# SSD scan of a hybrid decoder step: decays fetched after their exponential, differences on VectorE, GpSimd's weight remainders in pieces, three projections in a layer's first group

## The chip, the cores and the metric

The kernel runs on one core of a Trainium2 chip: TensorE (PE; its weight loads are PEld), VectorE (DVE), ScalarE (ACT), GpSimd (POOL) and SyncE (SP), which issues the DMAs. The metric is the device time in microseconds of one execution. The median of three runs of the kernel before is 2900.59 us (2896.8 to 2905.93).

## The reference

Two layers. Each layer takes 1024 prompt tokens and 32 sample tokens (8 sequences of 4), 1024 wide, through

```python
u = rms_norm(x, norm_mix)
q, k, v, z, xbc, dt = split(u @ w_in)              # 512, 128, 128, 1024, 1536, 16 columns
xbc = silu(causal_conv(xbc, width 4))              # x: 16 heads of 64;  B, C: 2 groups of 128 states
y = ssd_scan(x, softplus(dt + dt_bias), -exp(a_log), B, C, state) + d_skip * x
x = x + concat([attention(q, k, v), rms_norm(y * silu(z))]) @ w_out
x = x + (silu(g) * up) @ w_down                    # FFN, 2816 wide
```

The scan works in chunks of 128 tokens. Within a chunk, with `acum` the running sum of `dt * A` and s, q two tokens of it,

```python
decay   = exp(where(q >= s, acum[q] - acum[s], -inf))
y_intra = (C B^T * decay) @ (x * dt)
states  = B^T (x * dt * exp(acum[end] - acum));  h = h * exp(acum[end]) + states
y_inter = (C @ h_before) * exp(acum)
```

## The kernel before

Activations lie transposed: 128 columns of the model on the partitions, the 1056 tokens along the free axis in three tiles of 352. Each projection of 128 output columns is, for one tile, 8 (or 4, or 5) blocks k of three matmuls (`mm3`, L280 to L295): weights and activations are split into a high part rounded to fp32r and a low remainder, and hi·hi, hi·lo and lo·hi are added up in one PSUM bank of tag `g` (three of them). A tile of a projection is thus 24 matmuls of 128x352.

**Weights.** `load_next` (L252) fetches a block (tag `w`, 5 buffers), ScalarE casts it to `whi` (L266, 3 buffers), and GpSimd subtracts for the remainder (L267), in one instruction for all 8 blocks k. `weights(key)` keeps one weight prepared ahead.

**Order.** The program is written tile by tile; a planner orders the instructions of each engine with its own model of durations, and each engine then runs its queue in that order. `Flow` mixes the work around the projections: after each tile of a projection, `flow.tick()` advances one or two of the open generators by one `yield`. `issue_after` pins something behind a given instruction.

**Start.** The rows of x are fetched (L209), squared on ScalarE (L473), transposed on TensorE (L467) and copied out (L479), a reciprocal root is iterated on VectorE (`rsqrt`, L305 to L311), and per block k VectorE scales (L485), ScalarE casts to `ahi` (L486) and VectorE or GpSimd takes the remainder `alo` (L487; in tile 0 four of eight on GpSimd). This is written in the functions `roots`, `columns` and `first_norm`, the squares of tile 1 ahead of the norm of tile 0. In layer 1 the same comes from `norm_end` (L351 to L356, its splits at L244 and L248) behind the last down projection (L373).

**Projections.** `proj` (L556) takes one or more columns blocks and goes over the three tiles, all blocks of a tile before the next tile. The first group is dt (`d`, 16 columns, L289) with block x10 (C of group 0); then x8 (B of group 0) by itself; then x0, x1 and so on. A conv block leaves PSUM on ScalarE (L657), is weighted on ScalarE and VectorE (L667, L669), and gets its Silu on ScalarE (L670). A z block takes its Silu on ScalarE (L860), multiplies y on VectorE (L864), and squares on ScalarE (L868) with the sum on GpSimd (L869).

**Steps.** `steps` (L572, pushed behind the first group) computes softplus and the running sums; the transposed sums go to DRAM as `acd` (L613).

**Scan.** `ssd(j)`, j = 0 to 7 per layer, treats two heads in five `yield`s. In the first two, one for each half hf of 512 tokens: fetch `acd` of both heads broadcast over the partitions into `bc` (tag F1, 512 KB); transpose y (L728); two VectorE products with `wdec` and `dt` (L732); eight ScalarE Relus of 128x128 (L738), which make `max(acum[s] - acum[q], 0)` into `tt` (tag F2); its exponential (L739), the exponential of `bc` (L740, 128x1024), GpSimd's product of `bc` with C (L741, 128x1024), VectorE's product of `tt` with the masked C B^T (L742). The third computes the chunk states (matmuls L748) and the running state H (L753, L758). The fourth adds the intra part into a PSUM bank per half (L767, 64 stationary columns a head), the fifth adds the inter part into the same banks (L778, per chunk and head 64 columns of H against 128 columns of `bc`), and VectorE puts d_skip * x + PSUM into y (L780). TensorE shows two matmul records for each fp32 matmul.

After the scan: `stream` (the sample states, L832 to L846), `gnorm` (L872), `prep` (L685), attention (L1116 to L1260), the out projection (`one_ssm`, whose sum is L1271), and the FFN.

Of the kernel before, what the change touches and what calls it, by code (L numbers as in the profile page):

```python
# [10 lines left out]
F32 = mybir.dt.float32  # L11
# [7 lines left out]
L = 2  # L19
# [141 lines left out]
def body(ctx: ExitStack, tc, A, outs):  # L161
# [90 lines left out]
    def load_next():  # L252

        k, (fill, nk, cw) = wlist.popleft()
        raw = mk("w", [P, nk, cw], bufs=WB)
        load[0] = fill(raw)
        if cw == 16:

            both = mk("whi", [P, nk, 32], F32R, bufs=3)
            SC.copy(both[:, :, 0:16], raw)  # L260
            G.tensor_tensor(both[:, :, 16:32], raw, both[:, :, 0:16].bitcast(F32), op=ALU.subtract)
            wready[k] = both, None
            return
        hi = mk("whi", [P, nk, cw], F32R, bufs=3)
        lo = mk("w", [P, nk, cw], F32R, bufs=WB)
        SC.copy(hi, raw)  # L266
        G.tensor_tensor(lo, raw, hi.bitcast(F32), op=ALU.subtract)  # L267
        wready[k] = hi, lo
# [136 lines left out]
    acd = [dr.tile([16, S], F32, name=f"acd{l}") for l in range(L)]  # L405
# [53 lines left out]
    sizes = [[P if b < 8 else NS for b in range(3 * t, 3 * t + 3)] for t in range(NT)]  # L459

    def blocks(t):
        return slice(3 * t * P, 3 * t * P + sum(sizes[t]))

    def rows_to_columns(t, src):
        pt = pbank()
        for i, m in enumerate(sizes[t]):
            TE.transpose(pt[:, i * P:i * P + m], src(i)[0:m], ident[0:m, 0:m])  # L467
        return pt[:, 0:sum(sizes[t])]

    def roots(t):  # L470
        for i, m in enumerate(sizes[t]):
            sq = slot("F1", [P, D])
            SC.activation(sq[0:m], xr[3 * t + i][0:m], AF.Square, accum_out=s9[0:m, 3 * t + i:3 * t + i + 1])  # L473
        return rsqrt("r3", s9[:, 3 * t:3 * t + 3], D, bufs=2)

    def columns(t):
        for k in range(KD):
            pt = rows_to_columns(t, lambda i: xr[3 * t + i][:, k * P:(k + 1) * P])
            (SC.copy if k % 2 and t else V.tensor_copy)(x[k][:, blocks(t)], pt)  # L479

    def first_norm(t, y):
        SC.copy(rb[:, blocks(t)], rows_to_columns(t, lambda i: y[:, i:i + 1].to_broadcast([P, P])))
        for k in range(KD):
            s = mk("nu", [P, TW], bufs=3)
            V.scalar_tensor_tensor(s, x[k][:, tsl(t)], g_mix(0, k), rb[:, tsl(t)], op0=ALU.mult, op1=ALU.mult)  # L485
            hi = SC.copy(u[0][t][:, k, :], s)  # L486
            (V if k % 4 == 3 or (k % 2 and t == 0) else G).tensor_tensor(u[1][t][:, k, :], s, u[0][t][:, k, :].bitcast(F32), op=ALU.subtract)  # L487
        return hi

    y = roots(0)  # L490
    columns(0)
    y1 = roots(1)
    hi = first_norm(0, y)
    columns(1)

    with tc.issue_after(hi.ins):
        y2 = roots(2)
    first_norm(1, y1)
    columns(2)
    first_norm(2, y2)  # L500
# [54 lines left out]
    for l in range(L):  # L555
# [16 lines left out]
        def steps():  # L572
# [38 lines left out]
            acT = s2[:, 0:P]  # L611
            V.tensor_copy(acT, pt[:, 0:P])
            SY.dma_start(out=acd[l].rearrange("h (c q) -> (h c) q", q=P), in_=acT)  # L613
# [103 lines left out]
        def ssd(j):  # L717
# [3 lines left out]
            bcs, tts, xds, pys = {}, {}, {}, {}  # L721
            for hf in range(2):
                sl = slice(hf * 512, hf * 512 + 512)
                bc = bcs[hf] = slot("F1", [P, 2, 512])
                SY.dma_start(out=bc, in_=acd[l][2 * j:2 * j + 2, sl].partition_broadcast(P))
# [8 lines left out]
                tt = tts[hf] = slot("F2", [P, 2, 512])  # L734
# [26 lines left out]
            for hf in range(2):  # L761
                tt, xd2 = tts[hf], xds[hf]
                py = pys[hf] = pbank()
                for c in range(4):
                    q = slice(c * P, (c + 1) * P)
                    for hh in range(2):
                        TE.matmul(py[hh * 64:hh * 64 + 64, q], lhsT=xd2[:, 0, c, hh, :], rhs=tt[:, hh, q],  # L767
                                  start=(c == 0), stop=False)
            yield
            for hf in range(2):  # L770
                sl = slice(hf * 512, hf * 512 + 512)
                py, bc = pys[hf], bcs[hf]
                for c in range(4):
                    ci = hf * 4 + c
                    q = slice(c * P, (c + 1) * P)
# [117 lines left out]
        def z(j):  # L893
# [5 lines left out]
             conv(10, ct))  # L899
        flow.push("steps", steps())  # L900
        proj(conv(8, bt))
# [527 lines left out]
```

## Time and profile before

| | |
|---|---|
| median of three runs | 2900.59 us |
| the profiled execution | 2900.49 us |
| its span, first to last instruction | 2898.6 us |
| mean granted TensorE clock | 0.985 |
| busy PE, DVE, ACT, POOL | 2825.6, 1642.5, 1114.6, 983.5 us |

"Busy" is the time in which an engine has an instruction running. Matmuls are pipelined: a 128x352 record lasts about 0.32 us, while a new one starts every 0.16 us. A line such as L267 is a line of the kernel. `out<-in` names tiles by their tags, so `p` and `g` are PSUM banks, `F<-F` two tiles of the F slots.

The stages in the order of time are: start (0 to 70 us), layer 0's projections with scans (70 to 450), attention's queries and the mixing (450 to 650), FFN (650 to 1450), then the same for layer 1 from 1450 on.

### The profile page before, as it was taken

To read this page: it belongs to the slowest core of one execution; us is meant where nothing else is said; L and a number is where in the kernel's file an instruction comes from. 1 tells how busy PE (TensorE), PEld (TensorE's weight loads), DVE (VectorE), ACT (ScalarE), POOL (GpSimd) and SP (SyncE) were. 2 spreads that over 40 slices of the span, in tenths; PEclk is the share of its full clock that TensorE was granted. 3 is DMA by queue.
4 is the path that set the end of the run, shared out by engine and by line. 5 is a ranking of instruction groups with operands and counts; after the bars stand their busy time and mean duration, and the time that the engine had idled before them with its cause. 6 is when DMAs were issued, how large, how long until landed. Compare 5 with 4: busy or idle time off the path is not lost. (4 is left out here: it accounts for less than half of the span.)

```text
span 2898.6 us, 46682 instructions
## 1 busy us (share of the span) xinstructions
PE 2825.6 (97%) x18456; PEld 2725.1 (94%) x18456; DVE 1642.5 (57%) x3639; ACT 1114.6 (38%) x2326; POOL 983.5 (34%) x884
## 2 busy tenths in 40 slices
PE   7999999999999999999988999999999999999999
PEld 6989898889999999999988898988899999999999
DVE  7765648756348862333487565587553678523232
ACT  5775737644212111111247666476431121112121
POOL 4343337435222222222243333365442222222221
PEclk8999999999999999999999999999999999999999
DMA  4222222102123321211222212220021333111112
GB/s 170 90 83 66 73 67 98 33 17 72 39 61 106 96 87 37 59 34 55 75 90 73 86 46 90 63 99 19 26 73 34 88 92 117 56 48 45 52 37 82
DMA packets 308323, 197.78 MB, mean 68 GB/s; under 512 B 28255, under 2 KB 287623, under 8 KB 308073
## 3 DMA queue, kind: packets, MB, share of 16 engines
q1 hardware_dynamic: 308072, 194.79, 22.4%
q8 instruction: 146, 2.39, 0.3%
q14 instruction: 73, 0.59, 0.1%
q10 hardware_dynamic: 32, 0.01, 0.0%
HBM read 171.49 MB, written 25.30 MB: 68 GB/s over the span
## 5 line engine op out<-in xcount | busy, mean ns | idle before, releaser
L293 PE MATMUL g<-ahi,whi 128*128 128x352 f32 x3744 | 1229.2, 329 | 6.6 <-DVE big L1271 5.8
L295 PE MATMUL g<-ahi,w 128*128 128x352 f32 x3744 | 1219.3, 326 | 0.0
L294 PE MATMUL g<-alo,whi 128*128 128x352 f32 x3744 | 1217.9, 325 | 0.0
L267 POOL TENSOR_TENSOR w<-w,whi 128x1024 fp32r<-128x1024 f32 (+2 forms) x248 | 512.4, 2066 | 1207.6 <-ACT whi L266 954.1
L293 PEld LDWEIGHTS g<-ahi,whi 128*128 128x128 f32 x3744 | 710.9, 190 | 21.5 <-issue 12.0
L294 PEld LDWEIGHTS g<-alo,whi 128*128 128x128 f32 x3744 | 713.5, 191 | 8.1 <-issue 4.1
L295 PEld LDWEIGHTS g<-ahi,w 128*128 128x128 f32 x3744 | 713.0, 190 | 4.8 <-issue 4.1
L266 ACT CAST whi<-w 128x1024 fp32r<-128x1024 f32 (+2 forms) x248 | 225.4, 909 | 663.6 <-PE g L294 636.3
L295 PE MATMUL g<-A,w 128*128 128x352 f32 x1104 | 357.2, 324 | 0.0
L293 PE MATMUL g<-A,whi 128*128 128x352 f32 x1104 | 356.8, 324 | 0.0
L294 PE MATMUL g<-F,whi 128*128 128x352 f32 x960 | 310.0, 323 | 0.0
L373 DVE TENSOR_TENSOR big<-g,big 128x352 f32<-128x352 f32 x240 | 125.4, 522 | 235.7 <-PE g L295 235.4
L295 PEld LDWEIGHTS g<-A,w 128*128 128x128 f32 x1104 | 208.1, 188 | 0.0
L293 PEld LDWEIGHTS g<-A,whi 128*128 128x128 f32 x1104 | 207.7, 188 | 0.0
L1350 DVE SCALAR_TENSOR_TENSOR F<-F,xdds 128x128 f32<-128x128 f32 x512 | 201.6, 419 | 9.6
L1335 DVE TENSOR_TENSOR R<-R,g 128x352 f32<-128x352 f32 x132 | 68.9, 522 | 218.4 <-PE g L295 217.1
L294 PEld LDWEIGHTS g<-F,whi 128*128 128x128 f32 x960 | 181.0, 189 | 0.0
L1332 ACT ACTIVATE R<-R 128x352 f32<-128x352 f32 x132 | 65.6, 497 | 297.3 <-DVE R L1331 297.0
L244 ACT CAST A<-R 128x352 fp32r<-128x352 f32 x132 | 64.1, 486 | 282.2 <-DVE R L1335 281.0
L669 DVE SCALAR_TENSOR_TENSOR big<-R,vc,big 128x352 f32<-128x352 f32 (+2 forms) x240 | 138.2, 605 | 21.8 <-ACT big L667 21.0
L741 POOL TENSOR_TENSOR F<-F,A 128x1024 f32<-128x1024 f32 x32 | 83.5, 2610 | 111.7 <-ACT F L740 111.7
L1331 DVE TENSOR_TENSOR R<-g,sc 128x352 f32<-128x352 f32 x88 | 45.9, 521 | 125.6 <-PE g L295 122.9
(366 smaller groups left out, 3529.4 us busy)
## 6 DMA issues: line engine op xcount, KB each, us to landing
w<-in_w_gate_up_dram SPq DMA_DIRECT2D x88, 512.0 KB
w<-in_w_in_dram SPq DMA_DIRECT2D x44, 512.0 KB
F<-acd SPq DMA_DIRECT2D x32, 512.0 KB
out_dram<-F SPq DMA_DIRECT2D x42, 256.0 KB
w<-in_w_down_dram SPq DMA_DIRECT2D x32, 320.0 KB
w<-in_w_down_dram SPq DMA_DIRECT2D x40, 256.0 KB
xd<-big SPq DMA_DIRECT2D x16, 528.0 KB
big<-xd SPq DMA_DIRECT2D x16, 528.0 KB
```

The costliest lines, as they stand in the source:

```text
L244: SC.copy(hi, src)
L266: SC.copy(hi, raw)
L267: G.tensor_tensor(lo, raw, hi.bitcast(F32), op=ALU.subtract)
L293: TE.matmul(out, lhsT=hi[:, k, c], rhs=xh, start=(start and k == 0), stop=False)
L294: TE.matmul(out, lhsT=hi[:, k, c], rhs=xl, start=False, stop=False)
L295: TE.matmul(out, lhsT=lo[:, k, c], rhs=xh, start=False, stop=(stop and k == nk - 1))
L373: flow.anchor = V.tensor_tensor(d, pt[:, 0:TW], d, op=ALU.add)
L669: flow.anchor = V.scalar_tensor_tensor(d, r(w), c_w(l, w, m), d, op0=ALU.mult, op1=ALU.add)
L741: G.tensor_tensor(bc, bc, ct[:, sl].unsqueeze(1).to_broadcast([P, 2, 512]), op=ALU.mult)
L1332: SC.activation(sg[t], sg[t], AF.Silu)
L1335: flow.anchor = V.tensor_tensor(sg[t], sg[t], pt[:, 0:TW], op=ALU.mult)
L1350: V.scalar_tensor_tensor(st[:, jj, :], bb[:, t, :], xdds[:, j, b * 4 + t:b * 4 + t + 1], st[:, jj, :], op0=ALU.mult, op1=ALU.add)
```

## The change

- `load_next`: for all weights but those of the FFN, GpSimd's remainder is taken in pieces of two blocks k (128x256), four or two instructions in place of one.
- Start: the three functions are replaced by one plain loop over the tiles; the remainder is on VectorE for one of four k in every tile.
- `steps`: the exponential of the transposed sums is computed once, and both go to DRAM.
- `ssd`: the sums are fetched into `tt` (F1); VectorE computes `min(acum[q] - acum[s], 0)` in eight instructions; ScalarE keeps one exponential per half. The intra part goes into a bank of its own and is put into y at once. The inter part is C against the whole H (128 stationary columns, both heads in one matmul per chunk); VectorE multiplies it by the fetched exponential `ea` (F2, one per j, 512 KB in two fetches), and GpSimd adds it to y.
- First group: d, x10 and x8 in one `proj`; `steps` is pushed behind it.

```diff
@@ load_next
-        G.tensor_tensor(lo, raw, hi.bitcast(F32), op=ALU.subtract)
+        n = nk if k[1] in ("gu", "down") else 2
+        for a in range(0, nk, n):
+            G.tensor_tensor(lo[:, a:a + n], raw[:, a:a + n], hi[:, a:a + n].bitcast(F32), op=ALU.subtract)
@@ start: roots, columns, first_norm and their calls are replaced by
+    for t in range(NT):
...
+            SC.activation(sq[0:m], xr[b][0:m], AF.Square, accum_out=s9[0:m, b:b + 1])
...
+        y = rsqrt("r3", s9[:, 3 * t:3 * t + 3], D, bufs=1)
...
+            split(u[0][t][:, k, :], u[1][t][:, k, :], s, V if k % 4 == 3 else G)
@@ steps
-            SY.dma_start(out=acd[l].rearrange("h (c q) -> (h c) q", q=P), in_=acT)
+            SY.dma_start(out=acd[l][0].rearrange("h (c q) -> (h c) q", q=P), in_=acT)
+            SC.activation(eacT, pt[:, 0:P], AF.Exp)
+            SY.dma_start(out=acd[l][1].rearrange("h (c q) -> (h c) q", q=P), in_=eacT)
@@ ssd
+            ea = slot("F2", [P, S])
             for hf in range(2):
-                bc = bcs[hf] = slot("F1", [P, 2, 512])
-                SY.dma_start(out=bc, in_=acd[l][2 * j:2 * j + 2, sl].partition_broadcast(P))
+                tt = tts[hf] = slot("F1", [P, 2, 512])
+                SY.dma_start(out=tt, in_=acd[l][0, 2 * j:2 * j + 2, sl].partition_broadcast(P))
+                if hf:
+                    for hh in range(2):
+                        SY.dma_start(out=ea[hh * 64:hh * 64 + 64], in_=acd[l][1, 2 * j + hh].partition_broadcast(64))
...
-                        SC.activation(tt[:, hh, c * P:(c + 1) * P], bc[:, hh, c * P:(c + 1) * P], AF.Relu, bias=acum[:, cc:cc + 1], scale=-1.0)
-                SC.activation(tt, tt, AF.Exp, scale=-1.0)
-                SC.activation(bc, bc, AF.Exp)
-                G.tensor_tensor(bc, bc, ct[:, sl].unsqueeze(1).to_broadcast([P, 2, 512]), op=ALU.mult)
+                        d = tt[:, hh, c * P:(c + 1) * P]
+                        V.tensor_scalar(d, d, acum[:, cc:cc + 1], 0.0, op0=ALU.subtract, op1=ALU.min)
+                SC.activation(tt, tt, AF.Exp)
...
-                        TE.matmul(py[hh * 64:hh * 64 + 64, q], lhsT=xd2[:, 0, c, hh, :], rhs=tt[:, hh, q],
-                                  start=(c == 0), stop=False)
+                        TE.matmul(py[hh * 64:hh * 64 + 64, q], lhsT=xd2[:, 0, c, hh, :], rhs=tt[:, hh, q], start=True, stop=True)
+                V.scalar_tensor_tensor(y[:, sl], y[:, sl], dcol[:, j, l:l + 1], py, op0=ALU.mult, op1=ALU.add)
...
-                    for hh in range(2):
-                        if ci:
-                            TE.matmul(py[hh * 64:hh * 64 + 64, q], lhsT=H[:, ci - 1, hh * 64:hh * 64 + 64], rhs=bc[:, hh, q],
-                                      start=False, stop=(c == 3))
-                V.scalar_tensor_tensor(y[:, sl], y[:, sl], dcol[:, j, l:l + 1], py, op0=ALU.mult, op1=ALU.add)
+                    TE.matmul(py[:, c * P:(c + 1) * P], lhsT=H[:, ci - 1, :], rhs=ct[:, ci * P:(ci + 1) * P], start=True, stop=True)
+                V.tensor_tensor(ea[:, sl], py[:, 0 if hf else P:], ea[:, sl], op=ALU.mult)
+                G.tensor_tensor(y[:, sl], y[:, sl], ea[:, sl], op=ALU.add)
@@ the first group
-             conv(10, ct))
+             conv(10, ct), conv(8, bt))
         flow.push("steps", steps())
-        proj(conv(8, bt))
```

## Rows read from the trace of the kernel before

**Rows 1.** Windows: stage, length; busy (count) PE, PEld, DVE, ACT, POOL; clock; DMA share, GB/s.

```profile
0.00:70.00 70.00, 54.07 (x265) 43.42 (x266) 50.19 (x115) 36.71 (x73) 28.07 (x36) 0.83 0.51 176
100.00:230.00 130.00, 120.35 (x914) 111.67 (x913) 91.78 (x208) 90.07 (x185) 49.78 (x43) 0.97 0.28 80
230.00:390.00 160.00, 153.81 (x1145) 144.62 (x1144) 99.65 (x246) 100.82 (x199) 57.06 (x48) 0.99 0.27 79
650.00:1450.00 800.00, 800.00 (x4997) 799.85 (x4996) 396.43 (x769) 170.30 (x287) 221.43 (x143) 1.00 0.22 65
1450.00:1500.00 50.00, 42.99 (x264) 37.91 (x263) 41.09 (x89) 21.26 (x42) 25.62 (x21) 0.93 0.24 79
1540.00:1660.00 120.00, 110.28 (x843) 101.58 (x843) 82.23 (x192) 87.09 (x173) 45.68 (x36) 0.94 0.25 73
1660.00:1820.00 160.00, 153.25 (x1145) 144.15 (x1145) 97.40 (x246) 100.71 (x199) 56.35 (x46) 0.99 0.27 79
```

**Rows 2.** Waits of PE: total us, times, longest us.

```profile
PE p L748 <- DVE F L732: 14.9, 6, 4.5
PE g L293 <- DVE big L1271: 5.8, 2, 2.9
PE p L767 <- DVE F L742: 4.3, 1, 4.3
PE p L844 <- ACT nsq L840: 3.2, 4, 1.6
PE g L289 <- DVE alo L487: 3.2, 2, 2.0
PE g L289 <- DVE alo L248: 2.9, 1, 2.9
PE p L837 <- ACT sc L833: 2.7, 2, 1.9
PE p L876 <- POOL A L869: 2.5, 2, 1.2
```

**Rows 3.** Timeline, 196 to 216 us, ACT, DVE and PE: start, duration, [idle before].

```profile
196.06 4.80 ACT L738 ACTIVATE F<-F,acum 128x128 f32<-128x128 f32 x16
...
212.26 2.48 DVE L864 TENSOR_TENSOR big<-big,nu 128x320 f32<-128x320 f32 x1 [2.41 <-ACT nu L860]
...
214.77 0.68 DVE L732 TENSOR_TENSOR F<-p,wdec 128x512 f32<-128x512 f32 x1
...
215.50 1.40 PE L748 MATMUL p<-F,A 128*128 128x128 f32 x8 [4.46 <-DVE F L732]
```

**Rows 4.** Groups by form: count, busy us, mean ns, idle before.

```profile
L738 ACT ACTIVATE F<-F,acum 128x128 f32<-128x128 f32 x256 | 78.5, 390 | 29.4 <-DMA F<-acd 29.4
L740 ACT ACTIVATE F<-F 128x1024 f32<-128x1024 f32 x32 | 33.4, 1044 | 0.0
L741 POOL TENSOR_TENSOR F<-F,A 128x1024 f32<-128x1024 f32 x32 | 83.5, 2610 | 111.7 <-ACT F L740 111.7
L267 POOL TENSOR_TENSOR w<-w,whi 128x1024 fp32r<-128x1024 f32 x160 | 389.6, 2435 | 780.2 <-ACT whi L266 613.5 <-issue 165.0 <-POOL rc L665 0.8
L267 POOL TENSOR_TENSOR w<-w,whi 128x512 fp32r<-128x512 f32 x56 | 72.4, 1293 | 242.1 <-ACT whi L266 190.6 <-issue 51.5
L1348 DVE TENSOR_SCALAR F<-F,eends 128x128 f32<-128x128 f32 x128 | 60.7, 495 | 0.0
L748 PE MATMUL p<-F,A 128*128 128x128 f32 x256 | 35.0, 288 | 14.9 <-DVE F L732 14.9
L778 PE MATMUL p<-F,A 128*64 128x128 f32 x448 | 28.1, 276 | 0.0
```

**Rows 5.** Timeline, 498 to 502 us, POOL and DVE.

```profile
498.87 2.46 POOL L267 TENSOR_TENSOR w<-w,whi 128x1024 fp32r<-128x1024 f32 x1
...
499.17 2.38 DVE L310 SCALAR_TENSOR_TENSOR F<-F 128x192 f32<-128x192 f32 x1
```

**Rows 6.** Timeline of DVE at 850 us, the form L1348 undisturbed.

```profile
850.47 0.28 DVE L1348 TENSOR_SCALAR F<-F,eends 128x128 f32<-128x128 f32 x1
```

More of the change, by code (lines that the diff above doesn't have):

```diff
@@ L404, in body @@
     xd = [dr.tile([D, T], F32, name=f"xd{l}") for l in range(L)]
-    acd = [dr.tile([16, S], F32, name=f"acd{l}") for l in range(L)]
+    acd = [dr.tile([2, 16, S], F32, name=f"acd{l}") for l in range(L)]
     cbd = [dr.tile([2, NS, P], F32, name=f"cbd{l}") for l in range(L)]
@@ L457, in body, with rows_to_columns @@
     rb = slot("F2", [P, T])
[L459 to L471, printed above, removed]
-            sq = slot("F1", [P, D])
-            SC.activation(sq[0:m], xr[3 * t + i][0:m], AF.Square, accum_out=s9[0:m, 3 * t + i:3 * t + i + 1])
-        return rsqrt("r3", s9[:, 3 * t:3 * t + 3], D, bufs=2)
-    def columns(t):
+    for t in range(NT):
+        bs = range(3 * t, 3 * t + 3)
+        n = [P if b < 8 else NS for b in bs]
+        c0, w = 3 * t * P, sum(n)
+        for b, m in zip(bs, n):
+            sq = slot("F1", [P, D])
+            SC.activation(sq[0:m], xr[b][0:m], AF.Square, accum_out=s9[0:m, b:b + 1])
+        def rows_to_columns(src):
+            pt = pbank()
+            for i, m in enumerate(n):
+                TE.transpose(pt[:, i * P:i * P + m], src(i)[0:m], ident[0:m, 0:m])
+            return pt[:, 0:w]
         for k in range(KD):
[L478 to L482, printed above, removed]
+            pt = rows_to_columns(lambda i: xr[3 * t + i][:, k * P:(k + 1) * P])
+            (SC.copy if k % 2 and t else V.tensor_copy)(x[k][:, c0:c0 + w], pt)
+        y = rsqrt("r3", s9[:, 3 * t:3 * t + 3], D, bufs=1)
+        SC.copy(rb[:, c0:c0 + w], rows_to_columns(lambda i: y[:, i:i + 1].to_broadcast([P, P])))
         for k in range(KD):
@@ L485, in first_norm @@
             V.scalar_tensor_tensor(s, x[k][:, tsl(t)], g_mix(0, k), rb[:, tsl(t)], op0=ALU.mult, op1=ALU.mult)
[L486 to L500, printed above, removed]
+            split(u[0][t][:, k, :], u[1][t][:, k, :], s, V if k % 4 == 3 else G)
     vrow = slot("F1", [P, P])
@@ L610, in steps @@
             TE.transpose(pt[:, 0:P], acum, ident)
-            acT = s2[:, 0:P]
+            acT, eacT = s2[:, 0:P], s3[:, 0:P]
             V.tensor_copy(acT, pt[:, 0:P])
-            SY.dma_start(out=acd[l].rearrange("h (c q) -> (h c) q", q=P), in_=acT)
+            SY.dma_start(out=acd[l][0].rearrange("h (c q) -> (h c) q", q=P), in_=acT)
+            SC.activation(eacT, pt[:, 0:P], AF.Exp)
+            SY.dma_start(out=acd[l][1].rearrange("h (c q) -> (h c) q", q=P), in_=eacT)
             dts = dt[0:16, P:W]
@@ L720, in ssd @@
             H = slot("A4", [P, 8, P])
-            bcs, tts, xds, pys = {}, {}, {}, {}
+            tts, xds = {}, {}
+            ea = slot("F2", [P, S])
             for hf in range(2):
                 sl = slice(hf * 512, hf * 512 + 512)
-                bc = bcs[hf] = slot("F1", [P, 2, 512])
-                SY.dma_start(out=bc, in_=acd[l][2 * j:2 * j + 2, sl].partition_broadcast(P))
+                tt = tts[hf] = slot("F1", [P, 2, 512])
[3 more added lines that the diff above has]
+                        SY.dma_start(out=ea[hh * 64:hh * 64 + 64], in_=acd[l][1, 2 * j + hh].partition_broadcast(64))
                 px = pbank()
@@ L733, in ssd @@
                                     v.unsqueeze(3).to_broadcast([P, 4, 2, 64]), op=ALU.mult)
-                tt = tts[hf] = slot("F2", [P, 2, 512])
                 for hh in range(2):
@@ L761, in ssd @@
             for hf in range(2):
+                sl = slice(hf * 512, hf * 512 + 512)
                 tt, xd2 = tts[hf], xds[hf]
-                py = pys[hf] = pbank()
+                py = pbank()
                 for c in range(4):
@@ L766, in ssd @@
                     for hh in range(2):
-                        TE.matmul(py[hh * 64:hh * 64 + 64, q], lhsT=xd2[:, 0, c, hh, :], rhs=tt[:, hh, q],
-                                  start=(c == 0), stop=False)
+                        TE.matmul(py[hh * 64:hh * 64 + 64, q], lhsT=xd2[:, 0, c, hh, :], rhs=tt[:, hh, q], start=True, stop=True)
+                V.scalar_tensor_tensor(y[:, sl], y[:, sl], dcol[:, j, l:l + 1], py, op0=ALU.mult, op1=ALU.add)
             yield
             for hf in range(2):
-                sl = slice(hf * 512, hf * 512 + 512)
-                py, bc = pys[hf], bcs[hf]
-                for c in range(4):
+                sl = slice(hf * 512 if hf else P, hf * 512 + 512)
+                py = pbank()
+                for c in range(0 if hf else 1, 4):
                     ci = hf * 4 + c
-                    q = slice(c * P, (c + 1) * P)
-                    for hh in range(2):
-                        if ci:
-                            TE.matmul(py[hh * 64:hh * 64 + 64, q], lhsT=H[:, ci - 1, hh * 64:hh * 64 + 64], rhs=bc[:, hh, q],
-                                      start=False, stop=(c == 3))
-                V.scalar_tensor_tensor(y[:, sl], y[:, sl], dcol[:, j, l:l + 1], py, op0=ALU.mult, op1=ALU.add)
+                    TE.matmul(py[:, c * P:(c + 1) * P], lhsT=H[:, ci - 1, :], rhs=ct[:, ci * P:(ci + 1) * P], start=True, stop=True)
+                V.tensor_tensor(ea[:, sl], py[:, 0 if hf else P:], ea[:, sl], op=ALU.mult)
+                G.tensor_tensor(y[:, sl], y[:, sl], ea[:, sl], op=ALU.add)
             pt = pbank()
```

## The prediction

> **What bounds the kernel now.** I read the granted clock first (0.985 over the whole span, so little is lost to the slow level), then the windows by stage, then the waits of TensorE, and last the timelines of the places where it waited longest. The reader is to see in [rows 1] that TensorE is busy in 800.00 of 800 us of the FFN (4997 records, one each 0.16 us): nothing that the diff does can be felt there, except by moving it as a whole. The stages with scans are different. In the four stretches with `ssd` (100 to 390 and 1540 to 1820 us) TensorE is idle for 9.7, 6.2, 9.7 and 6.8 us, 32.4 us together, and the clock is below full. In the two starts it is idle for 15.9 of 70 and 7.0 of 50 us.
>
> What ends this idle time is in [rows 2]: in the scans `xd2` on VectorE (L732, 14.9 us), the masked product (L742, 4.3), two copies of `stream` on ScalarE (L840 3.2, L833 2.7) and GpSimd's sum of squares (L869, 2.5): 27.6 us in 15 waits. VectorE is named most often, but [rows 3] show who was late. ScalarE runs 16 Relus for 4.80 us, then two exponentials per half; a z block therefore gets its Silu (L860) late, VectorE's L864, which needs it, waits 2.41 us at the head of VectorE's queue, and the L732 behind it starts at 214.77. TensorE has stood 4.46 us for that. TensorE takes its queue in the order the planner wrote, so it doesn't go round such a wait. The scarce thing in a scan is thus the ScalarE queue in bursts (90.07 us of 130), with GpSimd's long products behind it.
>
> **The scans: what leaves ScalarE and GpSimd.** Per j, ScalarE loses the Relus, 78.5 us over 16 j = 4.9, and two exponentials of 1.04: 7.0 us, or 112 us over the kernel [rows 4]. GpSimd loses two products of 2.61 and gets two sums of 128x512, for which the remainder of that size stands (1.29): 5.2 out, 2.6 in. In 100 to 230 us, with four j, ScalarE falls from 90 to 62 us of 130. With that the five waits of the last paragraph lose their cause. All 27.6 us could go, and the half-speed stretches behind them: in the four windows the clock is short by 3.9, 1.6, 7.2 and 1.6 us (length times what is missing to 1.00), 14.3 in all, of which I put half, 7, on matmuls that ran slowly, the rest on the idle time itself. Best case -34.6 us.
>
> What comes in its place is on VectorE: 16 `tensor_scalar` of 128x128 per j. The same form stands in the FFN at L1348: 0.28 us undisturbed [rows 6], 0.495 on the mean [rows 4], where many of them wait. In a run of equal instructions starts come closer than durations (the Relus: 0.390 each, 78.5/256 = 0.307 per start, 0.79 of it), so 0.22 to 0.50 each, 3.5 to 7.9 us; and two products out of PSUM like L732 at 0.68. Together 4.9 to 9.3 us per j; I take 4.9, since the undisturbed row is the nearer one if GpSimd runs less. VectorE then has 91.8 + 4 x 4.9 = 111 us of 130 in the dense stretch (86%), before what it saves by no longer meeting L741. That is more than the ScalarE share that caused the waits, but without its lumps: two exponentials in one piece become 0.22 us pieces, and TensorE's `g` banks are emptied by ScalarE (L657, L860), not by VectorE. The fetch of the sums is waited for by ScalarE today, 29.4 us in 13 waits [rows 4]; that wait would move to the head of VectorE's queue, with conv taps (L669) behind it. But the slot F1 is now free after the intra matmuls (L767), one `yield`, so about one tile, before the inter matmuls (L778) that free it today; 29.4/13 = 2.3 us fits in a tile of 24 x 0.16 = 3.8 us, so I put it at nothing (29.4 us of VectorE's time if that cover is gone). The fetch of `ea` stands in SyncE's queue between the fetch of the second half and the next weights; F2 has two slots, and one j uses one, so it finds a free one. Taken for all of this: half of the best case, -17 us; bounds -35 and the slower rival below.
>
> The price of the new VectorE pieces hangs on one thing that [rows 5] show: GpSimd's L267 ran from 498.87 for 2.46 us, and an L310 on VectorE that started beside it took 2.38 us for 192 columns. The mean of L1348, 0.495 against 0.28, says that `tensor_scalar` meets such neighbours too. The Trainium skill (SBUF — State Buffer, "SBUF: two separate sides") states why: VectorE's second port pair is GpSimd's only one and is held exclusively for a whole instruction, where VectorE has two SBUF inputs or runs in a two-port mode; the Relus on ScalarE never met this. By that rule the new instructions pay 0.50 and the addition per j is 9.3 us, by the undisturbed row 4.9; [rows 4, 6] have both, and which holds in a scan no row shows.
>
> **The inter part on TensorE.** 448 records of 64 columns become 224 of 128 columns. The 448 take 28.1 us, 63 ns each, the L748 records of the new shape 35.0/256 = 137 ns [rows 4]: the two heads' halves run side by side today, so half as many matmuls are about as long. At 137 ns the new ones take 30.6 (+2.5), at 63 ns 14.1 (-14). I take +2: L748 is the same shape. The intra matmuls change only their flags: 0.
>
> **GpSimd's pieces.** From 1.293 us for 512 columns and 2.435 for 1024: 2.23 ns a column and 0.15 fixed, so 256 columns take 0.72 and four of them 2.89, +0.45 a weight; with 34 weights of eight blocks and 8 of four (+0.15) per layer 33 us over the kernel. GpSimd is busy in 50 of 130 us even in the dense stretch, so this is hidden, except in the mixing, where two such weights per layer stand in a full queue: 1.8 us if uncovered. On the other side stands TensorE's wait for L1271, 2.9 us twice [rows 2]: it is the L310 of [rows 5], and beside a piece it would wait 0.72 at most instead of 2.38, 1.7 us less in each layer. Taken -3, bounds -6 (wait gone altogether) and +2.
>
> **The starts.** Three products per tile give TensorE 8 matmuls of 0.16 us for each block k of u instead of 5, so a slow block is waited for less: the waits of L289 for `alo` are 3.2 and 2.9 us, and the two start windows are short of 11.9 and 3.5 us of clock, half of it again slow matmuls (7.7). Best case -13.8. Against it: `whi` has three slots, d, x10 and x8 fill them, so x0's cast can only start behind d's last matmul; cast (1.04, as L740) and a first piece 0.72 are 1.8 us per layer if TensorE has run dry by then. And in tile 0 of layer 0 six remainders are on GpSimd, two more than today, 0.93 each by the line above, 1.9 us. The squares of tile 1 come behind the norm of tile 0, which helps tile 0 and delays tile 1: no net. I take half of the gain and half of the cost of the cast: -5; bounds -14 and +5.5. `steps` starts when d is complete, as before; in the order it moves one projection back, and x0 fills the place of x8.
>
> **Sum**, against the profiled execution's own 2900.49 us (span 2898.6, 1.9 around it, 0.1 below the median 2900.59): 2900.5 - 17 + 2 - 3 - 5 = 2877.5 us.
>
> **Rivals.**
> *Everything goes*: all waits of the scans and their slow stretches (-34.6), best starts (-13.8), -3 and +2: 2851. For it: every one of the long waits leads back to ScalarE or GpSimd; against it: some will find a new releaser, because the planner's order rests on a model.
> *The waits change hands*: VectorE takes ScalarE's place, as many us of wait with another name; starts even, -3 +2: 2899.5. For it: 86% of VectorE is above the 69% of ScalarE that caused the waits.
> *VectorE becomes the bound in the dense scans (slower)*: place, L732 and the masked product, which TensorE's L748 and L767 wait for; the `tensor_scalar` runs stand behind GpSimd and behind the fetch. It decides when VectorE has no time left in 100 to 230 us: at 9.3 us per j it has 91.8 + 37 = 129 of 130. Then the addition of the eight dense j is on the path: 8 x 4.9 to 8 x 9.3 = 39 to 74 us, 7 us of slow clock stay, and 34.6 go: +11 to +46; with the 4.9 taken above 2912. Against it: GpSimd's longest products go, and with them a part of those 91.8 us.
> *Half the inter matmuls are half the time* would add -16 to the forecast, 2861; 63 against 137 ns speaks against it; it is inside the range.
>
> **Chances.** Forecast 0.55 (its own range 2862 to 2890), everything 0.13, change of hands 0.17, slower 0.15. What this kernel's measurement can tell from no change is 0.3%, 8.7 us, so faster is below 2891.9 and slower above 2909.3: faster 0.68 (forecast and everything), same 0.17, slower 0.15. Range for 8 in 10: 2850 to 2908; it leaves out the slower rival and a little of the best case.
>
> **What would show it.** Right: in 100 to 390 and 1540 to 1820 us TensorE's idle time falls from 32.4 to about half, ScalarE's share from 69% to about 50%, VectorE's rises to 80 to 86%; no wait of L748 for L732 over 3 us; the inter matmuls total 25 to 31 us; L310 beside L267 under 1 us; `alo` waits fall and a short wait for x0's `whi` appears. Wrong: L748 or the intra matmuls wait for VectorE in every j; the first `tensor_scalar` of a half waits for the fetch by 2 us or more; TensorE stands over 3 us at x0; or the FFN starts later than at 650 us.

## The result: 2827.9 us, three times the gain that was forecast

The changed kernel takes 2827.88 us (median of 4 runs, 2826.73 to 2830.64), the kernel before 2903.26 beside it: a ratio of 0.9743 (95% interval 0.9721 to 0.9765), 75 us less, where 23 were forecast. 2827.88 lies below the range of 2850 to 2908. One execution of e6 below (7531 us at a granted clock of 0.55) was a slow one and is in no comparison.

The span fell from 2898.6 to 2825.7 us. To see where, I cut each trace at the same work, by the count of TensorE's 352-column matmuls within a layer, and added up the times from one matmul's start to the next (us, worked out from all records):

| stage (352-column matmuls of a layer) | before | after | difference |
|---|---|---|---|
| start, 1 to 192, layer 0 and 1 | 78.1, 46.8 | 62.9, 42.7 | -15.2, -4.1 |
| scans, to 1560 | 326.4, 331.6 | 304.9, 303.8 | -21.5, -27.8 |
| attention's queries and first mixing, to 1920 | 154.1 for both | 152.0 | -2.1 |
| all the rest, FFN above all | 1953.2 for both | 1951.3 | -1.9 |

The scans gave 49.3 us and the starts 19.3. The 352-column matmuls that ran at half speed fell from 166 to 55.

Each column is one execution, and the short first stage differs between executions that run the same code there: kernels e1, e9 and e10 below, whose edits touch nothing ahead of `steps`, needed 72.5, 72.4 and 73.8 us for it, not 78.1. Up to 60 us their four engines run the same instructions in the same order. So 4 to 6 of the 15.2 us belong to this execution of the kernel before and not to the change.

The windows of the profile after, in the columns of [rows 1] and in the same stages, which now lie earlier:

```profile
0.00:60.00 60.00, 47.84 (x273) 39.09 (x274) 50.17 (x116) 36.56 (x73) 30.54 (x43) 0.91 0.60 206
80.00:200.00 120.00, 118.86 (x861) 112.48 (x860) 100.72 (x295) 72.81 (x127) 46.14 (x64) 1.00 0.39 113
200.00:352.00 152.00, 152.00 (x1125) 145.06 (x1125) 123.94 (x330) 67.36 (x122) 57.50 (x76) 1.00 0.32 93
610.00:1410.00 800.00, 800.00 (x4997) 799.81 (x4996) 394.62 (x766) 170.38 (x287) 222.47 (x148) 1.00 0.22 65
1410.00:1450.00 40.00, 37.61 (x236) 34.13 (x235) 32.32 (x79) 17.42 (x35) 19.90 (x22) 0.91 0.30 98
1490.00:1600.00 110.00, 107.92 (x807) 101.23 (x805) 93.48 (x277) 67.09 (x116) 44.20 (x58) 1.00 0.41 119
1600.00:1750.00 150.00, 149.87 (x1096) 143.32 (x1095) 116.03 (x313) 66.50 (x119) 58.61 (x73) 1.00 0.32 95
```

TensorE is idle for 1.1, 0, 2.1 and 0.1 us in the four scan windows, which were 32.4 in all, and the granted clock there is 1.00. VectorE is at 84% in the dense stretch (100.72 of 120), ScalarE at 61%. In the FFN TensorE's time is the same as before.

TensorE's waits of after, in the columns of [rows 2] (L473 is before's L467, L296 its L293, L1259 its L1271, L738 its L748, L723 its L732, L833 its L844):

```profile
PE p L473 <- DVE r3v L308: 7.0, 2, 4.9
PE g L296 <- DVE big L1259: 5.8, 2, 2.9
PE p L738 <- DVE F L723: 2.5, 2, 1.7
PE p L1000 <- ACT nsq L988: 1.2, 4, 0.5
PE p L833 <- ACT nsq L829: 0.6, 2, 0.3
PE g L292 <- DVE alo L248: 0.4, 1, 0.4
```

Of the 27.6 us in the scans 3.1 are left (L738 and L833). The mixing's wait (L1259), 5.8 us, is what it was.

The groups by form, which answer to [rows 4]:

```profile
L730 DVE TENSOR_SCALAR F<-F,acum 128x128 f32<-128x128 f32 x256 | 63.5, 322 | 25.5 <-DMA F<-acd 23.9 <-issue 1.6
L731 ACT ACTIVATE F<-F 128x1024 f32<-128x1024 f32 x32 | 33.7, 1060 | 11.7 <-DVE F L730 11.5
L769 POOL TENSOR_TENSOR big<-big,F 128x512 f32<-128x512 f32 x16 | 30.3, 1895 | 9.8 <-DVE F L768 9.8
L270 POOL TENSOR_TENSOR w<-w,whi 128x256 fp32r<-128x256 f32 x304 | 242.6, 827 | 282.3 <-ACT whi L266 176.7 <-issue 104.3 <-POOL rc L651 0.8
L270 POOL TENSOR_TENSOR w<-w,whi 128x1024 fp32r<-128x1024 f32 x92 | 220.9, 2401 | 525.5 <-ACT whi L266 437.5 <-issue 87.1 <-POOL R L1301 0.7
L768 DVE TENSOR_TENSOR F<-p,F 128x512 f32<-128x512 f32 x16 | 10.9, 680 | 0.0
L738 PE MATMUL p<-F,A 128*128 128x128 f32 x256 | 31.7, 275 | 2.5 <-DVE F L723 2.5
L767 PE MATMUL p<-A,A 128*128 128x128 f32 x224 | 27.6, 275 | 0.0
```

The differences (L730) cost VectorE 63.5/16 = 4.0 us per j. The wait for the fetch is still there, 23.9 us, and now VectorE has it. The inter matmuls (L767) are busy for 27.6 us, 28.1 before. A piece of a remainder takes 0.83 us on the mean; 200 of the 304 take 0.7, which is the price that the prediction worked out (0.72), and the others are longer.

One j of the dense stretch after, from its timeline (start, duration, idle before):

```profile
179.97 1.66 DVE L730 TENSOR_SCALAR F<-F,acum 128x128 f32<-128x128 f32 x8 [2.29 <-DMA F<-acd]
...
183.09 3.64 DVE L730 TENSOR_SCALAR F<-F,acum 128x128 f32<-128x128 f32 x8 [1.46 <-DMA F<-acd]
...
183.79 2.85 POOL L270 TENSOR_TENSOR w<-w,whi 128x256 fp32r<-128x256 f32 x4 [6.14 <-issue]
```

Eight differences take 1.66 us where GpSimd is quiet and 3.64 us beside four pieces of a remainder: 0.21 and 0.46 us each, near the two prices of the prediction (0.22 and 0.50), in one j. VectorE stood 2.29 and 1.46 us for the fetches at the head of its queue, and TensorE, which had a tile to work on, for neither.

### The profile page after: what moved, and what is told of

Same layout as the page of the kernel before. It is cut to its first block, busy times and chain, and to the rows that moved or that the text cites. A ratio compares the mean times of both kernels' runs of the same rounds, so it can differ in the third digit from the quotient of the medians.

```text
span 2825.7 us, 46551 instructions
## 1 busy us (share of the span) xinstructions
PE 2794.5 (99%) x18232; PEld 2706.5 (96%) x18232; DVE 1677.9 (59%) x3925; ACT 995.6 (35%) x2028; POOL 1002.0 (35%) x1106
## 4 chain that ended last, share of the span: by engine, by line
PE 89%; DVE 4%; ACT 1%; POOL 1%; issue 0%; DMA 0%; DVEq 0%; ACTq 0%
PE g L296 26%; PE g L298 26%; PE g L297 26%; PE p L1179 1%; PE p L1171 1%; DVE big L655 1%; PE p L758 1%; PE p L738 1%; PE p L767 1%; PE p L1155 1%; PE p L1156 0%; ACT nu L950 0%; PE p L821 0%; PE p L719 0%; DVE F L730 0%; PE p L826 0%
## 5 line engine op out<-in xcount | busy, mean ns | idle before, releaser
L296 PE MATMUL g<-ahi,whi 128*128 128x352 f32 x3744 | 1223.2, 327 | 6.4 <-DVE big L1259 5.8
L270 POOL TENSOR_TENSOR w<-w,whi 128x256 fp32r<-128x256 f32 (+3 forms) x468 | 565.7, 1227 | 1201.0 <-ACT whi L266 920.8
L296 PEld LDWEIGHTS g<-ahi,whi 128*128 128x128 f32 x3744 | 704.8, 188 | 19.1 <-issue 9.9
L296 PE MATMUL g<-A,whi 128*128 128x352 f32 x1104 | 356.7, 324 | 0.0
L296 PEld LDWEIGHTS g<-A,whi 128*128 128x128 f32 x1104 | 207.7, 188 | 0.0
L655 DVE SCALAR_TENSOR_TENSOR big<-R,vc,big 128x352 f32<-128x352 f32 (+2 forms) x240 | 134.1, 587 | 11.7 <-ACT big L653 11.0
L1321 DVE TENSOR_TENSOR R<-R,xs 128x352 f32<-128x352 f32 x44 | 94.8, 2154 | 31.6 <-ACT R L1320 31.6
```

What stands on the lines that cost most here:

```text
L270: G.tensor_tensor(lo[:, a:a + n], raw[:, a:a + n], hi[:, a:a + n].bitcast(F32), op=ALU.subtract)
L296: TE.matmul(out, lhsT=hi[:, k, c], rhs=xh, start=(start and k == 0), stop=False)
L655: flow.anchor = V.scalar_tensor_tensor(d, r(w), c_w(l, w, m), d, op0=ALU.mult, op1=ALU.add)
L1321: V.tensor_tensor(sg[t], sg[t], rinv[t], op=ALU.mult)
```

## The experiments

The size of each is its ratio to the kernel before, run on the same chip, times 2903 us; by that the changed kernel is at -75. The intervals are 3 to 7 us to either side, and the difference of two rows is known to some 8 us.

| kernel | ratio (95%) | us against before |
|---|---|---|
| scan part alone (e1) | 0.9880 (0.9863 to 0.9897) | -35 |
| all but the scan part (e2) | 0.9863 (0.9842 to 0.9883) | -40 |
| all but the pieces (e3) | 0.9823 (0.9803 to 0.9842) | -51 |
| all but three products (e4) | 0.9794 (0.9775 to 0.9814) | -60 |
| pieces alone (e5) | 0.9933 (0.9913 to 0.9952) | -19 |
| loop alone (e6, e13) | 0.9959, 0.9968 (0.9953 to 0.9982) | -12, -9 |
| after, Relus back on ScalarE (e7) | 0.9780 (0.9758 to 0.9801) | -64 |
| after, differences twice (e8) | 0.9807 (0.9790 to 0.9823) | -56 |
| differences alone (e9) | 0.9913 (0.9890 to 0.9936) | -25 |
| GpSimd's product in pieces, alone (e10) | 0.9974 (0.9965 to 0.9984) | -8 |
| after, second pass on ScalarE (e11) | 0.9758 (0.9741 to 0.9774) | -70 |
| after, still shorter pieces (e12) | 0.9733 (0.9718 to 0.9747) | -78 |
| three products alone (e14) | 0.9931 (0.9912 to 0.9949) | -20 |
| after, pieces of four blocks (e15) | 0.9768 (0.9750 to 0.9786) | -67 |

**The four parts, one left out or alone (e1 to e4).** e1 has the edits of `steps` and `ssd` alone, e2 all the others, e3 and e4 the whole change without this:

```diff
@@ e3: load_next as before
-        for a in range(0, nk, n):
-            G.tensor_tensor(lo[:, a:a + n], raw[:, a:a + n], hi[:, a:a + n].bitcast(F32), op=ALU.subtract)
+        G.tensor_tensor(lo, raw, hi.bitcast(F32), op=ALU.subtract)
@@ e4: the first group as before
-             conv(10, ct), conv(8, bt))
+             conv(10, ct))
         flow.push("steps", steps())
+        proj(conv(8, bt))
```

> The kernel before with the scan's part alone (fetched exponential, VectorE differences, C against the whole H). Theory (ScalarE's bursts of 7 us per j were the cause of the waits in the scans, and nothing else is needed to lose them): 44 to 54 us below before, 2849 to 2859. Rival 1 (VectorE held by GpSimd's whole-weight remainders is half of it, so the pieces are needed): 15 to 30 us below, 2873 to 2888.

> The changed kernel with the scan as before (pieces, plain start loop, three products stay). Theory: the starts' 19 us and 2 to 4 us of the mixing, so 18 to 25 us below before, and the waits of L748 for xd2 as long as before. Rival 1 (pieces): 35 us or more below before.

> The changed kernel with GpSimd's remainder in one instruction per weight again. Theory: within 6 us of the changed kernel, some of that in the mixing. Rival 1 (the tensor_scalar runs stand behind GpSimd's 2.4 us instructions, and only the pieces keep VectorE from becoming the bound): 15 to 40 us slower than the changed kernel.

> The changed kernel with dt and x10 in the first group and x8 by itself behind it, as before. Theory (three products fill the waits on the low parts of u): 10 to 16 us slower than the changed kernel, nearly all ahead of the first scan of either layer. Rival 2 (the plain start loop brings the starts' gain): 0 to 5 us slower.

The scan part gives 35 us alone, between what my theory and its rival had said, and 75 - 40 = 35 on top of the rest. My theory at this point, that ScalarE's bursts are the whole of the scans' gain, falls with e1, e2 and e3. TensorE's idle time in the scans was 36.0 us before and 4.2 after. The scan part alone leaves 15.7 (e1), the other edits without it 17.9 (e2), all but the pieces 11.3 (e3): it takes both. Without the pieces the change is 23 us smaller, half of it in the scans, and the long wait for L732 (there L720) is back:

```profile
PE p L735 <- DVE F L720: 7.3, 2, 3.9
```

e1, where ScalarE has no Relus and GpSimd no long products, shows what is left of this wait (L754 and L739 are before's L748 and L732):

```profile
111.48 2.95 DVE L671 SCALAR_TENSOR_TENSOR big<-R,vc,big 128x352 f32<-128x352 f32 x1
...
111.69 2.33 POOL L267 TENSOR_TENSOR w<-w,whi 128x1024 fp32r<-128x1024 f32 x1
...
114.36 0.68 DVE L739 TENSOR_TENSOR F<-p,wdec 128x512 f32<-128x512 f32 x1
...
115.09 1.22 PE L754 MATMUL p<-F,A 128*128 128x128 f32 x4 [4.57 <-DVE F L739]
...
PE p L754 <- DVE F L739: 7.6, 2, 4.6
```

A conv tap on VectorE (L671), 0.57 us by its median, takes 2.95 us beside a whole remainder, and TensorE stands 4.57 us, longer than at any such wait before. e2 has the opposite: with the Relus and the products, but in pieces, no wait of TensorE for `xd2` over 0.3 us is left, where I had expected all of it; instead TensorE waits for `stream`'s copy (before's L833, 2.7 us then):

```profile
PE p L821 <- ACT sc L817: 9.2, 4, 3.9
```

Which wait is named changes from kernel to kernel, so the idle time is the safer measure.

Leaving out the third product of the first group costs 15 us (e4), as expected.

**Pieces (e5, e15, e12).** e5 is the kernel before with the first edit of the change alone. e15 and e12 are the changed kernel with this:

```diff
@@ e15: pieces of four blocks
-        n = nk if k[1] in ("gu", "down") else 2
+        n = nk if k[1] in ("gu", "down") else 4
@@ e12: pieces of one block, and the sum L769 in pieces
-        n = nk if k[1] in ("gu", "down") else 2
+        n = nk if k[1] in ("gu", "down") else 1
...
-                G.tensor_tensor(y[:, sl], y[:, sl], ea[:, sl], op=ALU.add)
+                for a in range(sl.start, sl.stop, P):
+                    G.tensor_tensor(y[:, a:a + P], y[:, a:a + P], ea[:, a:a + P], op=ALU.add)
```

> The kernel before, with one edit: GpSimd's remainder L267 in pieces of two blocks (not gate, up and down). Theory: the pieces act in the scans, by letting VectorE and GpSimd's own other work in between, and are worth as much alone as on top of the rest (20 us there): 14 to 25 us faster than before, two thirds of it in the scans, TensorE's idle time there from 36 to under 27 us, and the waits of L748 for L732 down from 14.9 us by half. Rival: the pieces pay only once VectorE carries the differences, so alone they give the mixing's share alone: 0 to 7 us faster, scans within 4 us of before. A third reading, that more and shorter instructions cost GpSimd time that matters, would make it slower by 2 us or more.

> The changed kernel with GpSimd's remainders in pieces of four blocks (128x512, some 1.3 us) where it has pieces of two (128x256, 0.83 us); whole ones of eight (2.4 us) were 20 us slower. Theory (the longest single instruction sets the stall, in proportion above what a scan can absorb): 4 to 11 us slower than the changed kernel. Rival (any cut does, since VectorE gets in once per weight): within 3 us.

> The changed kernel, with GpSimd's remainder in pieces of one block (128x128 instead of 128x256) and its sum L769 in pieces of 128x128. Theory (the longest single GpSimd instruction sets the stall): little is left, TensorE is idle for 4 us in both scans: 1 to 5 us faster. Rival (the fixed part of an instruction, 0.15 us from before's rows, times 608 more pieces and 96 more sums, 106 us more on GpSimd, now weighs more): 1 to 8 us slower.

Alone they give 19 us, on top 23: the first theory, and not that they pay only beside the differences. Its split is not seen: in e5's profiled execution the start is 6.8 us shorter (but 5.6, 5.7 and 4.3 in e1, e9 and e10 without any edit there) and layer 0's scans 5.2, layer 1's nothing net: 4.0 us less idle time there, but 3 us more of matmuls at half speed. The wait for `xd2` (L732, here L735) fell from 14.9 us, longest 4.5, by less than the half that I expected, to

```profile
PE p L751 <- DVE F L735: 8.8, 5, 2.8
```

With whole remainders (2.4 us), pieces of four blocks (1.29) and of two (0.83) on the changed kernel: -51, -67 and -75 us; pieces of one block, with the sum cut too, are no different from two (-78, intervals overlap). GpSimd is busy 78 us more there; the expectation counted 608 more pieces and 96 more sums, the trace has 304 and 80. The length of one GpSimd instruction matters: four blocks against eight make 16 us, clear of the noise. Two against four make 7, which is not (some +-8 us), so the rival that any cut does is not excluded.

**VectorE for ScalarE (e7, e8, e9, e11).**

```diff
@@ e7: after, with the Relus on ScalarE
-                        V.tensor_scalar(d, d, acum[:, cc:cc + 1], 0.0, op0=ALU.subtract, op1=ALU.min)
-                SC.activation(tt, tt, AF.Exp)
+                        SC.activation(d, d, AF.Relu, bias=acum[:, cc:cc + 1], scale=-1.0)
+                SC.activation(tt, tt, AF.Exp, scale=-1.0)
@@ e8: after, with a second operation behind each difference
+                        V.tensor_scalar(d, d, 0.0, None, op0=ALU.min)
@@ e9: before, with its Relus and their exponential as
-                        SC.activation(tt[:, hh, c * P:(c + 1) * P], bc[:, hh, c * P:(c + 1) * P], AF.Relu, bias=acum[:, cc:cc + 1], scale=-1.0)
-                SC.activation(tt, tt, AF.Exp, scale=-1.0)
+                        V.tensor_scalar(tt[:, hh, c * P:(c + 1) * P], bc[:, hh, c * P:(c + 1) * P], acum[:, cc:cc + 1], 0.0, op0=ALU.subtract, op1=ALU.min)
+                SC.activation(tt, tt, AF.Exp)
@@ e11: after, behind the exponential L731
+                SC.copy(tt, tt)
```

> The changed kernel, with the 16 differences per j back on ScalarE as Relus (L730 as before's L738, the exponential with scale -1); nothing else. Theory of the prediction (ScalarE's bursts are what TensorE waited for): most of the scan part's gain goes, 15 to 30 us slower than the changed kernel, and TensorE waits again for L723 behind a late Silu, 5 us or more. Rival: GpSimd's long products and the second exponential were what counted, the Relus alone cost little: under 7 us slower. A second rival, that VectorE is now the nearer limit, would make this kernel faster than the changed one.

> The kernel before, with the 16 differences per j on VectorE (tensor_scalar, subtract and min) instead of ScalarE's Relus; both exponentials, GpSimd's 2.61 us products L741 and the inter matmuls stay. Theory (the parts add up; putting the Relus back in the changed kernel cost 12.6 us): 8 to 18 us faster than before. Rival (the differences on VectorE pay only with GpSimd's long products gone, since each may stand behind one): within 5 us of before, with VectorE's time lost beside L741 above the 7.8 us of 100 to 230 us before.

> The changed kernel, with every one of the 256 differences (L730) followed by a second tensor_scalar of the same size on the same tile (min with 0, which changes nothing): 82 us more for VectorE over the kernel at 0.32 us each, 5.2 us per j. Theory: VectorE has room in the scans (100.7 of 120 us busy in the dense stretch, TensorE idle only 4 us in both scans): 3 to 15 us slower. Rival (the slower case of the prediction: VectorE near its limit in the dense stretch): the dense eight j are bound by it, 8 times 5.2 less what room there is, 25 us slower or more, with TensorE waiting for L723 and L732 in nearly every j.

> The changed kernel, with ScalarE copying each masked tile's exponential onto itself once more (128x1024, 1.04 us, 32 times), the time of the exponential that the change took away: 33 us back on ScalarE, in the same place. Theory (a part of the scan's gain that is left beside the Relus' 12.6 us belongs to ScalarE's second exponential): 4 to 12 us slower. Rival (ScalarE at 62 of 120 us has room for it, the rest of the gain belongs to GpSimd's products and to the matmuls): within 4 us of the changed kernel.

The differences alone are worth 25 us, more than expected, and 11 on top of the rest (13 by the medians), between the theory's 15 to 30 and the rival's 7. With the Relus back ScalarE is at 71% and VectorE at 65% of the dense stretch, both below the 84% that VectorE has after, and yet TensorE's idle time in the scans is 12.3 us, where it was 4.2. It waits for `stream`'s copy L822 (before's L833), not for L723 as I had expected: that wait is 2.2 us, against 2.5 without the Relus. Window and wait of e7:

```profile
80.00:200.00 120.00, 116.79 (x831) 110.27 (x830) 78.31 (x209) 85.65 (x181) 39.16 (x58) 0.99 0.37 109
...
PE p L826 <- ACT sc L822: 8.3, 4, 3.7
```

The other way round, 256 more VectorE operations (62.9 us of their own, and L730 7.2 longer) cost 19 us, 0.27 of what they take. The window of e8 shows VectorE at 89%:

```profile
80.00:200.00 120.00, 117.55 (x847) 110.39 (x846) 107.03 (x343) 70.15 (x123) 39.36 (x58) 1.00 0.36 105
```

So VectorE had room, but not for nothing: 19 us is more than my theory's 3 to 15 and less than the rival's 25. A second pass of ScalarE costs 4 us, at the lower edge of what was expected and not told from nothing. (ScalarE stood at 73 of 120 us, not at the 62 that the expectation has.)

**GpSimd's long product (e10).** The kernel before, with L741 as four products of 128x256:

```diff
-                G.tensor_tensor(bc, bc, ct[:, sl].unsqueeze(1).to_broadcast([P, 2, 512]), op=ALU.mult)
+                for hh in range(2):
+                    for a in range(0, 512, 256):
+                        G.tensor_tensor(bc[:, hh, a:a + 256], bc[:, hh, a:a + 256], ct[:, hf * 512 + a:hf * 512 + a + 256], op=ALU.mult)
```

> The kernel before, with GpSimd's product L741 (128x1024, 2.61 us) as four of 128x256: the same work, about 1 us more of GpSimd per half. Theory (the length of one GpSimd instruction is what VectorE and through it TensorE pays for): 4 to 12 us faster than before, and the waits of L748 for L732 under 10 us. Rival (what GpSimd does in total counts, or the product was not in the way): within 4 us of before, or slower.

-8 us (-5 to -10), and the wait for `xd2` is down from 14.9 us:

```profile
PE p L750 <- DVE F L732: 6.6, 5, 2.6
```

TensorE's idle time in the scans fell by 6.4 us, to 29.6. The scans' own time fell by 2.4 only and the start's by 4.3, so this one trace does not show that all 8 us come from the length of the product.

With the differences' 25 and ScalarE's 4 this makes 37 of the scan part's 35. That settles no share, for the singles do not add up: with 11 for the differences it makes 23. The inter matmuls' own step, below, is 2.8 us less in all.

**The start (e6, e13, e14).** e6 and e13 are the kernel before with the plain loop in place of `roots`, `columns` and `first_norm`, e14 is before with three products alone:

```diff
@@ e14
-             conv(10, ct))
+             conv(10, ct), conv(8, bt))
         flow.push("steps", steps())
-        proj(conv(8, bt))
```

> The kernel before, with the plain loop over tiles at the start of layer 0 alone. Theory (parts add up): without the scan part the rest gave 41 us; less 20 for the pieces and 13 for three products, this leaves about 8 for the loop: 4 to 10 us faster, all of it in the first 80 us, where 78.1 us for the first 192 matmuls of 352 columns become 69 to 74. Rival: the loop is only an exchange of tile 0 for tile 1: within 3 us of before, and then the parts help each other.

> The kernel before with the plain loop at the start of layer 0 alone, a second time, for its trace. By the times of the first: 8 to 16 us faster. Theory: the gain lies in the first 80 us, where TensorE waits less for the norms and the clock recovers earlier; the first 192 matmuls of 352 columns take 6 us less or more. Rival: they take the same within 3 us, and the gain lies in the scans, by another order of the queues behind the start.

> The kernel before with three products in the first tile (d, conv 10 and conv 8 in one projection) alone. Theory (adds up as on top of the rest): 9 to 16 us faster, nearly all in the two starts, where the waits of L289 for alo shrink and the half-speed matmuls are fewer. Rival (without the loop the third product stands behind the same late tile): 0 to 6 us.

The rows come from e13, which repeats e6 for its trace. The loop gives 9 to 12 us by the times. In the trace the scans take no less than before, and the first 192 matmuls of 352 columns 69.1 us, against 78.1 in the trace of before but 72.4 to 73.8 with the same old start in e1, e9 and e10: 3 to 9 us. Three products give 20 alone, more than the 9 to 16 expected, and 15 on top of the rest; the starts are 65.1 and 42.4 us instead of 78.1 and 46.8. The windows from 40 to 80 us, first of before, then of e10 (the old start once more), then of e13, then of e14:

```profile
40.00:80.00 40.00, 37.49 (x201) 32.43 (x198) 30.93 (x64) 20.21 (x37) 19.95 (x25) 0.83 0.33 118
```

```profile
40.00:80.00 40.00, 37.33 (x227) 32.71 (x226) 34.53 (x71) 20.92 (x39) 21.29 (x25) 0.96 0.41 145
```

```profile
40.00:80.00 40.00, 38.88 (x247) 34.63 (x247) 34.12 (x60) 22.68 (x42) 24.36 (x26) 1.00 0.32 109
```

```profile
40.00:80.00 40.00, 40.00 (x247) 35.21 (x247) 36.00 (x77) 24.32 (x46) 24.31 (x27) 0.96 0.42 150
```

Before, TensorE stood six times between 24 and 48 us (0.6 to 2.0 us each), and its 352-column matmuls ran at half speed (1.2 GHz) from 34.5 to 36.5, 50.0 to 58.9 and 73.1 to 76.0 us, 47 of them. Behind 26 us one stop of over 0.3 us is left in e13 (0.6 us at 46) and one in e14 (0.9 us at 29); half speed ends at 33 us in both, but for five matmuls of e14 at 73 us. The stops themselves are a small part: idle time fell by 1.4 and 2.5 us, the stage by 9 and 13. But the half-speed stretch of before from 50.0 to 58.9 us can't be put down to the stops ahead of it: e10 has the same three between 41 and 49 us (0.94, 0.83 and 0.86 us; 0.78, 0.83 and 0.85 in before), and its clock stays at full speed from 37 to 68 us.

## Why the prediction was wrong

**The step that failed: "Taken for all of this: half of the best case, -17 us."** The scan part measured -35 alone and -35 on top of the rest, as much as the best case of -34.6. I halved that because "some will find a new releaser", and no row stood for the half: with the whole change TensorE's idle time in the scans is 4.2 us of 36.0.

The cause was named in part. ScalarE's bursts held TensorE up (e7, e9), but they were not all of it: with them and GpSimd's products gone 15.7 us of idle time were left (e1), and without the pieces 11.3 (e3). The other cause stood in [rows 3], which I read for L864's wait and not for its length of 2.48 us, where its median is 0.53. Beside it ran, in the same view,

```profile
212.05 2.35 POOL L267 TENSOR_TENSOR w<-w,whi 128x1024 fp32r<-128x1024 f32 x1
```

So some 2 of those 4.46 us were a whole remainder on GpSimd, not ScalarE. Of the 14.9 us of waits for L732 about 7 go back to VectorE operations that stood so beside one GpSimd instruction (L864 at 212, 368 and 1642 us beside L267, L655 at 114 us beside L741): an estimate, from their durations there less their medians (0.53 and 0.17 us), at most the whole of a wait.

The stages with scans gave 49.3 us in all, since the pieces act in them too: 31.8 us of idle time, 7.6 us of 352-column matmuls at half speed, near the 7 that were forecast, 2.8 us of inter matmuls, and 7.1 us spread over the small matmuls and the large ones next to them. That last part I can't assign.

**Pieces: -3 us forecast, 19 to 23 measured.** This is the second mis-sized term. I used the row of L310 beside L267 [rows 5] twice, to price the differences and to credit the mixing, and not where it weighed most: in the scans VectorE operations ahead of TensorE stood beside 2.4 us remainders. For the scans I counted only what the pieces cost GpSimd. In the mixing, the one place I credited, nothing was gained. The timeline of after there:

```profile
459.95 3.29 POOL L270 TENSOR_TENSOR w<-w,whi 128x256 fp32r<-128x256 f32 x4
459.98 0.92 DVE L314 SCALAR_TENSOR_TENSOR F<-F 128x192 f32<-128x192 f32 x1
...
461.79 0.87 DVE L312 TENSOR_TENSOR F<-F 128x192 f32<-128x192 f32 x1
462.70 0.76 DVE L313 SCALAR_TENSOR_TENSOR F<-F 128x192 f32<-128x192 f32 x1
463.21 1.04 POOL L952 TENSOR_TENSOR nu<-nu,F 128x352 f32<-128x352 f32 x1
463.38 0.51 DVE L1259 TENSOR_TENSOR big<-g,big 128x352 f32<-128x352 f32 x1
```

The four pieces follow each other without a gap, and each VectorE operation of the root is as long as one: 0.92, 0.87 and 0.76 us (L313 and L314 take 0.36 a little later, at 465 us), 2.55 together, where one L310 took 2.38. With pieces of four blocks the wait is 7.6 us (e15), of one block 4.7 (e12). I priced one operation beside one piece and forgot that a chain meets a piece at every link. That is the Trainium skill's rule again (SBUF — State Buffer, "SBUF: two separate sides": the shared port is held for a whole instruction), and both traces agree with it: 2.38 us beside a whole remainder of 2.46, 0.76 to 0.92 beside pieces of 0.83. Shorter instructions bound one wait and not the sum over a chain.

**The starts: -5 forecast, 19.3 in the two traces.** Of these 4 to 6 belong to the one execution of before, as e1, e9 and e10 show; some 14 are left. Two terms. Three products were mis-sized (15 to 20 us by the times), again by halving and by a cost for x0's cast that did not come (the wait is not among TensorE's waits of after). The loop I put at "no net"; it is worth 9 to 12 us by the times. Layer 0's first stage fell by 15.2, of it 3.6 idle time, 5.6 half speed of 352-column matmuls and 6.0 in the small ones; 3.7 of the 5.6 are the stretch from 50.0 to 58.9 us that e10 does not have.

**What held.** VectorE's share (80 to 86% forecast, 84%), no wait of L748 over 3 us (1.7), inter matmuls between 25 and 31 us (27.6 of busy time; taken +2, measured -0.5, and -2.8 by their steps). The differences at 4.9 us per j were 4.0, and L310 beside a piece stayed under 1 us. ScalarE's share did not come out (about 50% forecast, 61% in the dense stretch, 44% behind it). The fetch I put at nothing because it would fit in a tile: it does not (23.9 us of VectorE's time), so the reason was wrong, but TensorE did not wait for it, and the value was right by luck. The first difference of a half waited 2.29 us for its fetch, which the prediction had among its signs of being wrong: the sign came, and the time was not lost. The slower rival is refuted by the result, and e8 shows how far off it is: even at 89% VectorE passes on only a quarter of what is added. "Everything goes" (2851), at 0.13, was the nearest, and still 23 us short, mostly by the pieces.

**What stays open:** whether the parts add up within their intervals (the singles make 35 + 19 + 11 + 20 = 85 against 75; differences 25 alone, 11 on top), how the 7.1 us of small matmuls divide, and why the clock of before fell at 50 us of its start where e10's did not.

## What to carry to other kernels

When the long waits of the scarce engine lead back to bursts that the change removes, forecast that they go; a discount needs a row that names the next releaser. Read each line of such a chain for its duration as well as for its wait: an operation several times longer than its median has a cause of its own. Share does not show what holds an engine up: with ScalarE at 71% in lumps TensorE was idle for 12.3 us of the scans, with VectorE at 84% in pieces of 0.2 to 0.5 us for 4.2. Price a GpSimd instruction by what it holds up on VectorE and in every stage where the two meet, link by link of a chain. And before a short stage is compared by one trace of each kernel, look at other kernels that run the same code there.

## What the runs showed of the hardware

Two fp32 matmuls of 64 stationary columns each, one per head, run side by side: before's 448 L778 records start in pairs some 6 ns apart, a pair each 0.1 us, and step by 62 ns on the mean; 224 of the full 128 columns step by 111 ns (27.6 and 24.8 us in all), so half as many were not half the time. GpSimd's sum of 128x512 (L769) takes 1.90 us on the mean, its remainder of the same size 1.29 [rows 4], which I had used as its price. The price was right: the shortest of the 16 sums takes 1.27 us, and the longest, 2.2 to 3.3 us, run beside VectorE's L732 of 128x1024, a product of two tiles. So the waiting goes both ways. And the granted clock need not be the same after the same work: in two starts with the same order of instructions, and three stops of 0.8 to 0.9 us at the same places, it was at half speed from 50.0 to 58.9 us in before and at full speed there in e10.
